# Moving the start addresses of an encoder kernel's SBUF tiles to multiples of 512 bytes

## The chip, the core and the metric

The kernel runs on one core of a Trainium2 chip. Five engines work side by side and are kept in step by semaphores: TensorE (PE in the profile, with its weight loads shown apart as PEld), VectorE (DVE), ScalarE (ACT), GpSimd (POOL) and SyncE (SP, which here only issues DMAs). TensorE reads two operands from SBUF, the on-chip memory of 128 partitions: a *stationary* operand of 128 columns, which a weight load brings in, and a *moving* operand of up to 512 columns, which is then streamed past it. The result goes to PSUM. The metric is the device time of one execution in microseconds, the median of several runs.

## The reference

Two layers over 512 positions of width 1024, in float32. Layer 0 mixes the positions with a stick-breaking attention, layer 1 with a gated linear recurrence (RG-LRU); each is followed by an MLP with a squared ReLU.

```python
for layer in range(2):
    h = rms_norm(x, norm_mix[layer])
    if layer == 0:
        y = stick_breaking_attention(h, w_qkv, w_o)   # 16 heads of 64
    else:
        y = rglru_block(h, w_in, conv_w, conv_b, w_a, b_a, w_x, b_x, lam, w_o)
    x = x + y
    h = rms_norm(x, norm_mlp[layer])
    u = relu(h @ w1[layer])                           # 1024 -> 4096
    x = x + (u * u) @ w2[layer]                       # 4096 -> 1024
return rms_norm(x, norm_final)
```

The attention weight of key k for query q is sigmoid(z) at k times the product of sigmoid(-z) over the keys between k and q. The recurrence is h[t] = a[t] h[t-1] + b[t] with gates computed from 16 diagonal blocks of 64 x 64. Nearly all of the arithmetic is in the dense products with the weight matrices.

## The kernel before

Activations lie with the features on the partitions: a chunk is 128 features by 512 positions, 8 chunks make the model width. Every float32 operand of a product is split into a high half, rounded to the TensorE format float32r, and a low half, the rest. A product is then three matmuls into the same PSUM bank: high times high, high times low, low times high (`three`, L217 to L221). ScalarE makes the high half of a weight tile (a cast, `wh`), VectorE the low half (a subtraction, `wl`), and DMAs on the SP queue, with some on POOL's, bring the raw weights.

The stages follow each other on TensorE in an order written out by hand. On the other engines a scheduler that works on estimated times sets the order of the instructions, save where the code chains them one behind the other. The stages are:

- Layer 0's mixer (to about 235 us): query and key projections with a moving operand of 512 positions (`xgh`, `xgl`, the halves of the normalised input) against weight slabs `wh`, `wl` (L219 to L221, L424); value projections in which the weight slab is the moving operand, 256 columns wide (L475 to L477); scores (`kh`, `kl` moving, `q` stationary, L559 and L560), transposes of the weights `w` with the identity as the moving operand (L600), values (`th`, `tl` moving, `v` stationary, L626 and L627); the output projection.
- The MLP of each layer by Strassen-Winograd's seven products in blocks, in four quarters. The quarters' *up* products (`Mlp.up`, L965) stream activations 256 columns wide past 128 columns of weights; the *down* products (`Mlp.times`, L1060) stream weights 512 columns wide past activations (`bh`, `bl`, or the split squares `sh`, `sl`). VectorE adds the block sums of weights, makes the low halves and gathers the results.
- Layer 1's mixer (about 566 to 720 us): input projections, convolution, gates, the scan on VectorE, the output projection.

SBUF is handed out by pools, in the order in which the pools are opened and, in a pool, in the order in which tags first occur. A tile starts on a multiple of 32 bytes. Pool `const` stands first; in it the one-column tile `eps_t` (L117) comes before the four 16 KB tiles `xgh`, `xgl`, `bh` and `bl`, and eight tiles of 8 columns (`lams`, L244) come behind them. `wpool` (raw weights, `wh`, `wl`), `work` (among others the small `rt`, `rc`, `rp`, `rn`, `rr`), `home`, and then the pools of each stage follow. So each small tile shifts the start of all that is allocated behind it:

| tiles | start, modulo 512 bytes, before | modulo 256 |
|---|---|---|
| `xgh`, `xgl`, `bh`, `bl` (every slice of them that a matmul takes) | 32 | 32 |
| `raw`, `wh`, `wl`, and all 2 KB tiles of `work` | 288 | 32 |
| `home` (also the tiles named `low`), `q`, `kh`, `kl`, `th`, `tl`, `v`, `w`; in layer 0's MLP `s41`, `sh`, `sl`; the gate weights | 480 | 224 |
| in layer 1's MLP `s41`, `sh`, `sl` (behind two small tiles of pool `last`) | 128 | 128 |
| `lasth`, `lastl` (behind the scan tiles, which are 513 columns wide) | 64 | 64 |
| `ones`, `ident` | 0 | 0 |

All slices that a matmul takes of a tile lie whole multiples of 512 bytes apart, so that each has its tile's number.

Of the kernel before, what the change touches and what calls it, by code (L numbers as in the profile page):

```python
# [11 lines left out]
F32 = mybir.dt.float32  # L12
F32R = mybir.dt.float32r
AF = mybir.ActivationFunctionType
# [3 lines left out]
P = 128  # L18
S = 512
D = 1024  # L20
C = D // P
# [40 lines left out]
def hybrid_encoder(  # L62
# [23 lines left out]
    nc = tc.nc  # L86
    V, A, G, PE = nc.vector, nc.scalar, nc.gpsimd, nc.tensor

    const = ctx.enter_context(tc.tile_pool(name="const", bufs=1))
    wpool = ctx.enter_context(tc.tile_pool(name="wpool", bufs=4))  # L90
    work = ctx.enter_context(tc.tile_pool(name="work", bufs=2))
# [5 lines left out]
    def bank(tag=None):  # L97
        if tag is None:
            tag = TAGS[turn[0] % len(TAGS)]
            turn[0] += 1  # L100
        return psum.tile([P, S], F32, tag=tag, name=f"ps_{tag}")

    def f(ap):
        return ap.bitcast(F32)
# [9 lines left out]
    V.memset(ones, 1.0)  # L114
    ident = const.tile([P, P], F32, tag="ident", name="ident")
    make_identity(nc, ident)
    eps_t = const.tile([P, 1], F32, tag="eps", name="eps_t")  # L117
    V.memset(eps_t, EPS)

    xgh = const.tile([P, C, S], F32R, tag="xgh", name="xgh")  # L120
# [5 lines left out]
    def halves(gname, c, xc):  # L126

        g = col(gname)[:, c : c + 1]
        A.activation(xgh[:, c, :], xc, AF.Identity, scale=g)
        return V.scalar_tensor_tensor(  # L130
            xgl[:, c, :], xc, g, f(xgh[:, c, :]), ALU.mult, ALU.subtract
        )
# [8 lines left out]
    class Squares:  # L141
# [21 lines left out]
        def inv_squares(self, ps):  # L163

            for t in range(S // P):
                PE.matmul(
                    ps[:, t : t + 1], self.acc[:, t * P : (t + 1) * P], ones[:, 0:1],
                    start=True, stop=True,
                )
            n = S // P  # L170
            rr = work.tile([P, 2 * n], F32, tag="rr", name="rr", bufs=1)
            V.tensor_scalar(rr[:, :n], ps[:, :n], 1.0 / D, EPS, ALU.mult, ALU.add)
            V.reciprocal(rr[:, :n], rr[:, :n])
            V.tensor_scalar(rr[:, n:], rr[:, :n], -1.0, None, ALU.mult)
            return rr
# [55 lines left out]
    def beside(ws, ah, al, pss, at, ks=range(C)):  # L231
# [9 lines left out]


    lams = {
        n: const.tile([P, C], F32, tag=f"lam_{n}", name=n)  # L244
        for n in ("ab", "pp", "den", "s1", "s2", "pl", "c8", "c4")
    }
    c8, c4 = lams["c8"], lams["c4"]
# [31 lines left out]
    NB = S // P  # L279
    PAIRS = H // 2  # L280
    half = [slice(0, HD), slice(HD, P)]
    so, early = {}, {}
# [7 lines left out]
    with ExitStack() as actx:  # L290
        hp = actx.enter_context(tc.tile_pool(name="hp", bufs=2))
        sp = actx.enter_context(tc.tile_pool(name="sp", bufs=1))
# [6 lines left out]
            fill=1.0, base=0, channel_multiplier=1,  # L299
        )  # L300

        scans = []
        for i in range(3):
            sc = sp.tile([P, S + 1], F32, tag=f"scan{i}", name=f"scan{i}")
            G.memset(sc[:, S : S + 1], 1.0)
            scans.append(sc)

        lasts = []
        for i in range(2):
            both = []  # L310
            for nm in ("h", "l"):
                t = sp.tile([P, 2 * P], F32R, tag=f"last{nm}{i}", name=f"last{nm}{i}")
                G.memset(f(t[:, :P]), 0.0)
                both.append(t)
            lasts.append(both)

        q, kh, kl, v, w = {}, {}, {}, {}, {}
        norm = {}
# [22 lines left out]
        def first_halves(pq, pk):  # L341

            qh, ql = parted(pq, "x")
            h = hp.tile([P, S], F32R, tag="th", name="th", bufs=3)
            l = hp.tile([P, S], F32R, tag="tl", name="tl", bufs=3)
            A.copy(h, pk)
            V.tensor_tensor(l, pk, f(h), ALU.subtract)
            q[0], kh[0], kl[0] = [], [], []
            for j in range(2):
                for tag, two, to in (("q", (qh, ql), q), ("kh", (h, h), kh), ("kl", (l, l), kl)):  # L350
                    t = hp.tile([P, S], F32R, tag=f"{tag}{j}", name=f"{tag}{j}")
                    for a, part in zip(half, two):
                        nc.sync.dma_start(out=f(t[a, :]), in_=f(part[half[j], :]))
                    to[0].append(t)
# [38 lines left out]
        others = {getattr(mybir.EngineType, e) for e in ("Activation", "DVE", "Pool", "SP")}  # L393
        with tc.manual_schedule(engines=others):
            A.dma_start(out=colt, in_=cols)
            A.activation(work.tile([P, 1], F32, tag="rt", name="early"), eps_t, AF.Sqrt)
            for j in range(2):
                parts[j][2](1, A)
            for c in range(C):
                nc.sync.dma_start(out=xcs[c], in_=xT[:, c, :])  # L400
                if c in (0, 3, 5):
                    for j in range(2):
                        parts[j][2]((c + 1) // 2)
            for j in range(2, 6):
                for i in range(2):
                    parts[j][2](i)

            parts[0][3](0, V.tensor_copy)
            for kind, c in START:
                if kind == "x":  # L410
                    halves("mix0", c, xcs[c])
                elif (kind, c) == ("q", 0):
                    parts[0][3](c, None)
                elif kind != "s":
                    parts["qknm".index(kind)][3](c)
                else:
                    A.activation(sqs[c], xcs[c], AF.Square)
                    if c:
                        V.tensor_tensor(sums, sums, sqs[c], ALU.add)

            for k in range(C):
                for n, (low, y) in enumerate(((0, xgh), (0, xgl), (1, xgh))):
                    for i in range(2):
                        PE.matmul(  # L424
                            first[i], parts[i][low][:, k, :], y[:, k, :], start=k == n == 0,
                            stop=k == C - 1 and n == 2,
                        )
            first_halves(*first)

        def inverse():  # L430

            pc = bank("z")
            for t in range(NB):
                PE.matmul(
                    pc[:, t : t + 1], sums[:, t * P : (t + 1) * P], ones[:, 0:1],
                    start=True, stop=True,
                )
            rc, rp, rn = (work.tile([P, NB], F32, tag=n, name=n, bufs=1) for n in ("rc", "rp", "rn"))
            diag = work.tile([P, S], F32, tag="sq", name="diag")
            with tc.high_priority():  # L440
                norm["root"] = A.activation(rc, pc[:, :NB], AF.Sqrt, bias=eps_t, scale=1.0 / D)
                V.reciprocal(rc, rc)
                for t in range(NB):
                    ts = slice(t * P, (t + 1) * P)
                    V.tensor_scalar(diag[:, ts], ident, rc[:, t : t + 1], None, ALU.mult)
                V.tensor_scalar(rp, rc, SCALE, None, ALU.mult)
                V.tensor_scalar(rn, rc, -SCALE, None, ALU.mult)
            norm.update(rc=rc, rp=rp, rn=rn)
            yield
            pr = bank("z")  # L450
            PE.matmul(pr, ones, diag, start=True, stop=True)
            r = work.tile([P, S], F32, tag="r", name="r")
            with tc.high_priority():
                norm["copy"] = A.copy(r, pr)
            norm["r"] = r
            yield
# [921 lines left out]
    with ExitStack() as rctx:  # L1378
# [155 lines left out]
        def root(c):  # L1534
            OA.activation(om[c], om[c], AF.Sqrt)
# [18 lines left out]
        def out_low(c):  # L1554
# [4 lines left out]
            "N": rms, "r": inverse, "R": gate_raw, "W": gate_high, "X": gate_low, "G": gates,  # L1559
            "n": scaled, "b": first_tap, "t": taps, "h": high, "l": low, "s": sigmoids,  # L1560
            "m": gated_input, "T": tanh, "E": exp, "d": decay, "q": root, "k": recur,
            "z": gate, "g": gelu, "y": times_gate, "u": out_high, "i": out_low,
        }
# [21 lines left out]
    with ExitStack() as mctx:  # L1585
        lp = mctx.enter_context(tc.tile_pool(name="last", bufs=1))
# [26 lines left out]

        A.activation(lp.tile([P, 1], F32, tag="rt", name="early"), eps_t, AF.Sqrt)

        ss = lp.tile([P, NB, 3], F32, tag="ss", name="ss")
        bias = lp.tile([P, NB], F32, tag="bias", name="bias")

        def square(t, h, i, cols=slice(0, S), end=False):
# [17 lines left out]
            EG.tensor_tensor(y, y, gb[h][:, cols], ALU.mult)  # L1637

        def root(t, i):
            rt = work.tile([P, 1], F32, tag="rt", name="rt")  # L1640
            A.activation(rt, ss[:, t, i : i + 1], AF.Sqrt, bias=bias[:, t : t + 1], scale=1.0 / D)
            V.reciprocal(rt, rt)
            return rt
# [24 lines left out]
        def end(ws, xs):  # L1668
            EG.turn(True)
            for t in range(2):  # L1670
                square(t, 0, 0)
                scaled(t, 0)
                square(t, 1, 1, end=True)
                rt = root(t, 1)
                one(t, 0, rt)
                both(t, 1, rt, last=mlp.gained)
# [6 lines left out]
            mlp.collect("P4", 0, xs[0])  # L1683
            square(2, 0, 1, end=True)
            two = root(2, 1)
            mlp.collect("P4", 1, xs[1])
            parts = [slice(i * HS, (i + 1) * HS) for i in range(2)]
# [86 lines left out]
```

## Time and profile before

| what | value |
|---|---|
| median of 3 runs | 1043.36 us (1043.2 to 1043.92) |
| span of the profiled execution | 1041.3 us, so the median lies 2.1 us above it |
| TensorE busy | 1032.1 us, 99% of the span, 5862 matmul records |
| VectorE, ScalarE, GpSimd busy | 858.7 us, 702.3 us, 171.8 us |
| granted TensorE clock, mean | 0.999 |
| HBM read | 137.41 MB |

The page gives no own time of the profiled execution beside its span. A matmul's record is longer than its turn on the engine: records overlap, since the next one begins to stream while the last one drains. The 512-column matmuls have records of about 390 ns but begin 227 to 234 ns apart. How long TensorE is held is therefore read from starts: from the chain of work, whose pieces give a start, a length and a count, or from the busy time of one source line over the whole span, divided by its count.

### The profile page before, as it was taken

The numbers are of one execution on the slowest core, as the hardware profiler recorded it, in microseconds if no ns is written. First come the engines' busy times: TensorE is split into PE (matmuls) and PEld (weight loads), VectorE is DVE, ScalarE is ACT, GpSimd is POOL, SyncE is SP. The second block draws the span as 40 slices with busy tenths as digits, with TensorE's granted clock in tenths as the row PEclk, the third lists the DMA queues.
The fourth block names the chain that finished last, engine by engine and source line by source line (L and its number), as shares of the span: only waits on it lengthen the run. The fifth ranks groups of instructions, "written<-read, shape, count | busy, mean of one in ns | idle before, by whom it ended". The sixth has DMA issues, their size and how long they took to land.

```text
span 1041.3 us, 15858 instructions
## 1 busy us (share of the span) xinstructions
PE 1032.1 (99%) x5862; PEld 902.2 (87%) x5862; DVE 858.7 (82%) x1148; ACT 702.3 (67%) x1083; POOL 171.8 (17%) x239
## 2 busy tenths in 40 slices
PE   9999999999999999999999999999999999999997
PEld 7988888888888988988988888888888988988986
DVE  7888787848788898898899888984789797897897
ACT  6777676826766773773775799964755773773865
POOL 0444444420010010010011121200000010010012
PEclk9999999999999999999999999999999999999999
DMA  7745454528546667567682675453346667667663
GB/s 243 216 111 143 117 151 102 162 88 297 137 81 189 182 137 211 161 136 209 162 209 76 159 176 142 102 222 101 82 87 173 180 138 206 161 137 200 145 129 107
DMA packets 53260, 160.46 MB, mean 154 GB/s; under 512 B 6720, under 2 KB 8256, under 8 KB 53184
## 3 DMA queue, kind: packets, MB, share of 16 engines
q1 hardware_dynamic: 42096, 120.35, 35.5%
q0 software_dynamic: 10656, 38.80, 22.5%
q8 instruction: 46, 0.75, 0.3%
q10 hardware_dynamic: 432, 0.31, 0.1%
q14 instruction: 30, 0.25, 0.1%
HBM read 137.41 MB, written 4.19 MB: 136 GB/s over the span
## 4 chain that ended last, share of the span: by engine, by line
PE 96%; ACT 2%; DMA 1%; DVE 1%; issue 0%; POOL 0%; ACTq 0%; DVEq 0%
PE ps_t L1060 17%; PE ps_acc L965 10%; PE ps_acc L1060 8%; PE ps_z L965 8%; PE ps_acc L221 5%; PE ps_acc L219 5%; PE ps_acc L220 5%; PE ps_o L965 5%; PE ps_z L1060 4%; PE ps_t L219 2%; PE ps_t L220 2%; PE ps_t L221 2%; PE ps_o L219 2%; PE ps_o L220 2%; PE ps_o L221 2%; PE ps_z L221 2%
## 5 line engine op out<-in xcount | busy, mean ns | idle before, releaser
L754 ACT CAST wh<-b 128x1024 fp32r<-128x1024 f32 x168 | 174.1, 1047 | 126.1 <-DVE b L754 71.5
L754 DVE TENSOR_TENSOR wl<-b,wh 128x1024 fp32r<-128x1024 f32 x168 | 203.5, 1220 | 48.4 <-ACT wh L754 47.9
L1042 POOL DMA_DIRECT2D b<-in_w_dn x40 | 35.0, 874 | 364.3 <-DVE b L754 204.4
L219 PE MATMUL ps_acc<-xgh,wh 128*128 128x512 f32 x192 | 78.5, 409 | 0.0
L221 PE MATMUL ps_acc<-xgl,wh 128*128 128x512 f32 x192 | 75.2, 391 | 0.0
L220 PE MATMUL ps_acc<-xgh,wl 128*128 128x512 f32 x192 | 75.1, 391 | 0.0
L578 DVE TENSOR_TENSOR_SCAN scan<-keep,later 128x128 f32<-128x128 f32 (+1 forms) x64 | 59.9, 939 | 16.9 <-ACT keep L568 9.8
L214 DVE TENSOR_TENSOR wl<-raw,wh 128x512 fp32r<-128x512 f32 (+2 forms) x70 | 61.5, 906 | 14.9 <-ACT wh L212 14.8
L754 ACT ACTIVATE u<-u 128x512 f32<-128x512 f32 x100 | 63.1, 632 | 5.5 <-DVE u L754 3.8
L212 ACT CAST wh<-raw 128x512 fp32r<-128x512 f32 (+2 forms) x70 | 50.6, 758 | 20.6 <-PE ps_acc L221 7.3
L582 POOL TENSOR_TENSOR w<-w,scan 128x128 f32<-128x128 f32 (+1 forms) x64 | 51.9, 812 | 56.7 <-DVE scan L578 53.3
L1042 POOL DMA_DIRECT2D b<-in_w_up x24 | 20.8, 868 | 240.2 <-DVE b L754 71.8
L754 DVE TENSOR_TENSOR b<-b,b 128x1024 f32<-128x1024 f32 x48 | 58.7, 1222 | 1.3
L754 DVE TENSOR_TENSOR u<-u 128x512 f32<-128x512 f32 (+1 forms) x92 | 54.8, 596 | 2.7 <-ACT u L754 1.1
L965 PE MATMUL ps_z<-xgh,wh 128*128 128x256 f32 x192 | 54.2, 282 | 0.0
L965 PE MATMUL ps_z<-xgh,wl 128*128 128x256 f32 x192 | 54.1, 282 | 0.0
L754 ACT CAST wh<-raw 128x1024 fp32r<-128x1024 f32 x46 | 48.0, 1047 | 8.7 <-PE ps_acc L1060 6.7
L965 PE MATMUL ps_acc<-low,wh 128*128 128x256 f32 x192 | 53.9, 281 | 0.0
L1060 PE MATMUL ps_t<-wl,sh 128*128 128x512 f32 x126 | 50.1, 398 | 0.0
L1060 PE MATMUL ps_t<-wh,sh 128*128 128x512 f32 x126 | 49.7, 395 | 0.0
L1060 PE MATMUL ps_t<-wh,sl 128*128 128x512 f32 x126 | 49.5, 393 | 0.0
L1060 PE MATMUL ps_t<-wh,bh 128*128 128x512 f32 x126 | 49.3, 391 | 0.0
(399 smaller groups left out, 3420.7 us busy)
## 6 DMA issues: line engine op xcount, KB each, us to landing
b<-in_w_dn SPq DMA_DIRECT2D x48, 512.0 KB, 4.4
b<-in_w_dn POOLq DMA_DIRECT2D x40, 512.0 KB, 5.7
b<-in_w_up SPq DMA_DIRECT2D x36, 512.0 KB, 4.5
b<-in_w_up POOLq DMA_DIRECT2D x24, 512.0 KB, 5.5
raw<-in_w_m SPq DMA_DIRECT2D x16, 512.0 KB, 4.5
raw<-in_w_dn SPq DMA_DIRECT2D x16, 512.0 KB, 4.7
raw<-in_w_in SPq DMA_DIRECT2D x16, 512.0 KB, 3.8
raw<-in_w_qk SPq DMA_DIRECT2D x12, 512.0 KB, 3.7
```

Source lines behind the costliest of these rows:

```text
L212: A.copy(wh[:, k, :], raw[:, k, :])
L214: V.tensor_tensor(wl[:, k, :], raw[:, k, :], f(wh[:, k, :]), ALU.subtract)
L219: PE.matmul(ps, wh, ah, start=start, stop=False)
L220: PE.matmul(ps, wl, ah, start=False, stop=False)
L221: PE.matmul(ps, wh, al, start=False, stop=stop)
L578: V.tensor_tensor_scan(sc[:, S - n : S][:, ::-1], keep[:, :n][:, ::-1], later[:, S - n :][:, ::-1], 1.0, ALU.mult, ALU.max,)
L582: G.tensor_tensor(wt, wt, sc[:, S - n + 1 : S + 1], ALU.mult)
L754: ins = getattr(self.e, name)(*args, **kwargs)
L965: PE.matmul(ps[:, i * HS : (i + 1) * HS], m, y, start=new and i == k == n == 0, stop=i == 1 and k == C // 2 - 1 and n == 2, skip_group_che ...
L1042: G.dma_start(out=unit[b].rearrange("p j n -> p (j n)"), in_=unit["src"](to), accum_op=ALU.add)
L1060: PE.matmul(ps, m, y[:, jj, cols], start=first and n == 0, stop=last and n == 2, skip_group_check=not new,)
```

## The change

A pool `small` is opened ahead of `const` and takes the small tiles: `eps_t`, the eight `lams`, `rt`, `rc`, `rp`, `rn`, `rr`. `eps_t` is made 16 columns wide, of which the first is used, and `ss` in the last stage 104 columns wide, of which the first 12 are used; both widths only fill up the pool to a multiple of 512 bytes at which the next tile begins. The 513-column scan tiles are allocated behind `lasth` and `lastl` and not in front of them. In the built program every operand of every matmul, moving or stationary, then starts on a multiple of 512 bytes: each number of the table above becomes 0. No size of a computation, no buffer count and no wait changes.

```diff
+    small = ctx.enter_context(tc.tile_pool(name="small", bufs=1))
     const = ctx.enter_context(tc.tile_pool(name="const", bufs=1))
...
-    eps_t = const.tile([P, 1], F32, tag="eps", name="eps_t")
+    eps_t = small.tile([P, 16], F32, tag="eps", name="eps_t")[:, :1]
...
-            rr = work.tile([P, 2 * n], F32, tag="rr", name="rr", bufs=1)
+            rr = small.tile([P, 2 * n], F32, tag="rr", name="rr")
...
     lams = {
-        n: const.tile([P, C], F32, tag=f"lam_{n}", name=n)
+        n: small.tile([P, C], F32, tag=f"lam_{n}", name=n)
...
-        scans = []
-        for i in range(3):
-            sc = sp.tile([P, S + 1], F32, tag=f"scan{i}", name=f"scan{i}")
-            G.memset(sc[:, S : S + 1], 1.0)
-            scans.append(sc)
-
         lasts = []
...
                 both.append(t)
             lasts.append(both)
+
+        scans = []
+        for i in range(3):
+            sc = sp.tile([P, S + 1], F32, tag=f"scan{i}", name=f"scan{i}")
+            G.memset(sc[:, S : S + 1], 1.0)
+            scans.append(sc)
...
-            A.activation(work.tile([P, 1], F32, tag="rt", name="early"), eps_t, AF.Sqrt)
+            A.activation(small.tile([P, 1], F32, tag="rt", name="early", bufs=2), eps_t, AF.Sqrt)
...
-            rc, rp, rn = (work.tile([P, NB], F32, tag=n, name=n, bufs=1) for n in ("rc", "rp", "rn"))
+            rc, rp, rn = (small.tile([P, NB], F32, tag=n, name=n) for n in ("rc", "rp", "rn"))
...
-        ss = lp.tile([P, NB, 3], F32, tag="ss", name="ss")
+        ss = lp.tile([P, 104], F32, tag="ss", name="ss")[:, : 3 * NB]
+        ss = ss.rearrange("p (t i) -> p t i", t=NB)
...
-            rt = work.tile([P, 1], F32, tag="rt", name="rt")
+            rt = small.tile([P, 1], F32, tag="rt", name="rt", bufs=2)
```

The one place where instructions move is POOL at the program's start, where it fills tiles with constants. On PE, DVE, ACT and SP the instructions and their order are the same in both kernels. Before, POOL's row from the fill of `later` (the mask of later keys) to the first multiplication by a scan stood so:

```order
L296 MEMSET later_100 128x512
L305 MEMSET scan0_105 128x1
masks.py:199 ISA
masks.py:199 AFFINE_SELECT ident_70<-ident_70 128x128
L305 MEMSET scan1_107 128x1
L305 MEMSET scan2_109 128x1
L313 MEMSET lasth0_111 128x128
L313 MEMSET lastl0_113 128x128
L313 MEMSET lasth1_115 128x128
L313 MEMSET lastl1_117 128x128
L297 AFFINE_SELECT later_100<-later_100 128x128
```

In the changed kernel the same stretch of POOL's row is:

```order
L297 MEMSET later_103 128x512
L308 MEMSET lasth0_108 128x128
masks.py:199 ISA
masks.py:199 AFFINE_SELECT ident_73<-ident_73 128x128
L308 MEMSET lastl0_110 128x128
L308 MEMSET lasth1_112 128x128
L308 MEMSET lastl1_114 128x128
L315 MEMSET scan0_116 128x1
L315 MEMSET scan1_118 128x1
L315 MEMSET scan2_120 128x1
L298 AFFINE_SELECT later_103<-later_103 128x128
```

The three one-column fills of the scan tiles now stand behind the four fills of `lasth` and `lastl`, and the identity is made one fill later; the row is of the same length.

## The prediction

> **What bounds the kernel now.** I read the page first, then the waits, the chain of work, and last the rows in order of time inside steady stretches.
>
> ```profile
> span 1041.3 us, 15858 instructions
> ...
> PE 1032.1 (99%) x5862; PEld 902.2 (87%) x5862; DVE 858.7 (82%) x1148; ACT 702.3 (67%) x1083; POOL 171.8 (17%) x239
> ...
> PE 96%; ACT 2%; DMA 1%; DVE 1%; issue 0%; POOL 0%; ACTq 0%; DVEq 0%
> ```
>
> TensorE is busy for 99% of the span and is 96% of the chain. Its own waits are these three:
>
> ```profile
> PE ps_acc L424 <- ACT xgh L129: 1.1, 1, 1.1
> PE ps_z L381 <- DVE eps_t L118: 1.1, 1, 1.1
> PE ps_z L965 <- ACT u L754: 0.6, 1, 0.6
> ```
>
> They come to 2.8 us, so the end is set by the sum of the matmuls' turns. The change touches those turns alone: where operands start. Is a turn's length a matter of the start? Pieces of the chain (start, us, what and how many) in six steady stretches, in each of which all moving operands and all stationary ones have the same two starts:
>
> ```profile
> 330.56 2.52 PE ps_acc L965 x21
> ...
> 333.56 2.27 PE ps_acc L965 x20
> ...
> 800.59 4.64 PE ps_acc L965 x39
> ...
> 772.73 2.49 PE ps_t L1060 x11
> ...
> 470.12 2.06 PE ps_acc L1060 x9
> ...
> 775.22 2.57 PE ps_t L1060 x11
> ```
>
> Divided by their counts, with the starts (modulo 256 bytes) of moving and stationary operand behind:
>
> - 256 columns: 120.0 ns (32 and 32, `xgh` past `wh`); 113.5 (224 and 32, layer 0's `s41` and `low` past `wh`); 119.0 (128 and 224 by turns, and 32, the same lines in layer 1)
> - 512 columns: 226 ns (32 and 32, `wh` past `bh`); 229 (32 and 224, `wh` past layer 0's `sh`); 234 (32 and 128, `wh` past layer 1's `sh`)
>
> The same source line, with the same shapes and with nothing to wait for, runs 113.5 or 119.0, 229 or 234, as its tiles lie. So the start matters, by 3 to 6% of a turn; the tiles' order in memory is a term of the time.
>
> What is the term made of? At equal starts (32 and 32) the two sizes differ by 226.5 - 120.0 = 106.5 ns for 256 columns, 0.416 ns a column; what is left is 13.3 ns a matmul, at both sizes the time of 32 columns. At 224 and 32 the rest is 113.5 - 106.5 = 7 ns, the time of 16 columns. Sixteen float32 columns are 64 bytes. An operand that begins 32 bytes past a multiple of 64, as all moving operands in these rows but layer 1's `s41` do, reaches into one 64-byte piece more than its length needs, 33 for 32 or 17 for 16. I read the 7 ns as that piece, and the second 7 ns as the moving stream meeting the weight load, since the next weights are read in the same time:
>
> ```profile
> 330.64 0.28 PE L965 MATMUL ps_acc<-xgh,wh 128*128 128x256 f32 x1
> 330.64 0.19 PEld L965 LDWEIGHTS ps_acc<-xgh,wl 128*128 128x128 f32 x1
> ```
>
> That reading is an inference from the six pieces. No stretch has both operands on a multiple of 64, so the state after the change isn't in this trace. The nearest thing is the transposes, whose moving operand `ident` starts at 0 (128 columns of float32, stationary `w` at 224):
>
> ```profile
> 59.05 0.60 PE L600 MATMUL ps_t<-ident,w 128*128 128x128 f32 x4
> ...
> L600 PE MATMUL ps_t<-ident,w x160: 270/272/327, 50.3 to 228.5; 128*128 128x128 f32 x160
> ```
>
> Four of them in 0.60 us, of which the last takes 0.272: (0.60 - 0.272) / 3 = 109 ns each. If float32 streams at half the rate, that is 106.5 ns and a rest of 2.5, well under 7.
>
> **The change part by part.** *Moving the small tiles to the front* adds and removes no instruction; their readers are the same. A column tile's start could matter to VectorE and ScalarE, but neither is waited for, beyond 0.6 us at L965. *Behind the scan tiles*, POOL's fills change places at the program's start:
>
> ```profile
> 1.42 0.10 POOL L305 MEMSET scan<- 128x1 f32 x1
> ...
> 2.44 0.29 POOL L297 TENSOR_SCALAR_AFFINE_SELECT later<-later 128x128 f32<-128x128 f32 x1
> 32.17 0.29 POOL L572 TENSOR_SCALAR_AFFINE_SELECT w<-w 128x128 f32<-128x128 f32 x1 [29.44 <-ACT w L567]
> ```
>
> All fills are over by 2.7 us and POOL then idles for 29.44 us. ScalarE's first write to a scan tile is a square made from `x`, after the first chunk has come; the fills keep their sum, so this costs nothing. Without that cover it would be the 0.2 us of a fill or two. *DMAs* land at other addresses in the same order; between 30 us and the last stage TensorE waits for none.
>
> *Every matmul's start* is the whole of the term. TensorE's time by line over the span, and for L219 to L221 the first and last of fifteen turns:
>
> ```profile
> 0.00:1041.30 1041.30, 239.53 (x2016) 239.18 (x2016) 1.00 0.58 154
> ...
> 0.00:1041.30 1041.30, 311.16 (x1356) 252.24 (x1356) 1.00 0.58 154
> ...
> 18.58 0.23 PE ps_t L219
> ...
> 21.98 0.23 PE ps_t L219
> ...
> L475 PE MATMUL ps_acc<-wh,xgh 128*128 128x256 f32 x112 | 32.4, 289 | 0.0
> ```
>
> The first row is L965 alone (2016 turns, 118.8 ns), the second L1060 alone (1356, 229.5 ns); 21.98 - 18.58 over 15 is 226.7 ns for the 3 x 496 projections; the value projections (3 x 112 of the last row's kind) have the first piece's starts, 120.0 ns.
>
> What do they cost at starts of 0 and 0? From below: the fixed part falls to the transposes' 2.5 ns, 109 and 216 ns. From above: nothing of the fixed part is tied to the piece, and equal starts are the worst relation, 120 ns and, by the worst steady piece, 234. I take the middle, by the row that the new state is nearest to: 32 and 32, the one with equal starts. It loses its extra piece (7 ns) and keeps its meeting with the weight load (6.7): 113.3 and 220.0 ns. Then:
>
> - L1060: 1356 x (229.5 - 220.0) = 12.9 us
> - L219 to L221: 1488 x (226.7 - 220.0) = 10.0 us
> - L965: 2016 x (118.8 - 113.3) = 11.1 us
> - L475 to L477: 336 x (120.0 - 113.3) = 2.3 us
>
> Together 36.3 us; scores, values and transposes, some 500 turns with smaller or unknown differences, are left out.
>
> Who is late next? VectorE, in the down products. Two such stages, and an up stage ahead of them (PE, PEld, DVE, ACT, POOL busy):
>
> ```profile
> 330.00:370.00 40.00, 40.00 (x340) 39.88 (x340) 33.09 (x35) 31.46 (x42) 3.48 (x4) 1.00 0.63 159
> 370.00:408.00 38.00, 38.00 (x168) 31.09 (x167) 35.76 (x41) 19.89 (x25) 4.35 (x5) 1.00 0.77 186
> ...
> 838.00:877.00 39.00, 39.00 (x172) 31.69 (x171) 36.30 (x42) 20.67 (x26) 4.37 (x5) 1.00 0.76 184
> ```
>
> At 220 ns the second takes 38.0 x 220.0 / 229.5 = 36.4 us, and VectorE's 35.76 are 98% of it. I charge 0.3 us of stalls to each of the seven full down stages, 2 us. The profiled execution's span of 1041.3 becomes 1007; the median lies 2.1 us above that span, so the forecast is 1043.4 - 36.3 + 2 = **1009 us**.
>
> **The rivals.** *The whole rest goes.* At 216 and 109.2 ns the same four lines give 18.3 + 15.9 + 19.4 + 3.6 = 57 us. But a down stage can't become shorter than VectorE's work in it: 38.0 - 35.76 = 2.2 us is to be had in each, about 13 us of L1060's 18.3 less some stalls. 50 us are left, 993. For it speaks the transposes' row, against it that they stream slower and so meet the weight load less. The Trainium skill, page "TensorE: Matmul & The Clock Gate", section "Wait — 56ns, not 53.3ns?", has this as the rule for back-to-back matmuls: columns over 2.4 GHz and about 2.5 ns more, 215.7 ns at 512. The trace agrees on the slope (0.416 ns a column) and disagrees on the rest, which is 7 to 20 ns in the six pieces; by that rule the time would be this rival's.
>
> *Nothing changes*: only the distance between the two operands counts, not where they start. Equal starts are what 32 and 32 is already; then all goes to 226.7 and 120.0. L1060 gains 1356 x 2.8 = 3.8 us, L965 loses 2016 x 1.2 = 2.4, the other lines stand: 1042. For it speaks that the most frequent relation of before has equal starts; against it the next rows. The Trainium skill, page "SBUF — State Buffer", section "Specifications (TRN2)", gives lines of 16 bytes, each new one at a price. All starts of before are multiples of 32 already, so by that rule there is nothing to align. The trace disagrees, since the layout modulo 256 moves the turn by 5 ns.
>
> *It becomes slower*: with equal starts both streams ask for the same place at once, and 32 and 32 escapes it only by its half piece. Four matmuls in a row at 224 and 224 (values and scores, 512 columns):
>
> ```profile
> 54.80 0.23 PE ps_o L626
> 55.03 0.24 PE ps_o L627
> 55.27 0.23 PE ps_z L559
> 55.50 0.23 PE ps_z L560
> ```
>
> (55.50 - 54.80) / 3 = 233 ns at equal starts, not 226. At 233 and 120 the lines lose 1356 x 3.5 + 1488 x 6.3 + 2016 x 1.2 = 4.7 + 9.4 + 2.4 = 16.5 us: 1060. It decides if the mean turn of 512 columns comes out above its present (311.16 + 1488 x 0.2267) / 2844 = 228.0 ns with the 256-column ones unmoved. Against it: those four stand in a mixed stretch, and their moving operands cut a 64-byte piece as well.
>
> **How the numbers follow.** Forecast (piece gone, meeting stays, 1000 to 1020): 0.36. Rest gone as well (985 to 1000): 0.27. Nothing changes (1038 to 1046): 0.12. Slower (1046 to 1062): 0.25. What a measurement can tell from no change is 0.2%, 2 us; of the third case I count about half as that, the rest as faster or slower by a little. So faster 0.67, same 0.06, slower 0.27. The range 988 to 1053 leaves out the lowest tip of the second case and more than half of the last, some 0.2. Over the two faster cases alone it would be 988 to 1020.
>
> **What would show it.** Right: L219 to L221 begin 220 ns apart, L965 113 ns, and layer 1's down products run like layer 0's; the chain's pieces in each stage are of one cadence; VectorE is above 95% in the down stages, with single waits of TensorE on `wl` at L1060. If the turns are 216 and 109, the rest went too. If they are 227 and 120, only the distance counts. If 512 columns take 233 or more, equal starts collide. The forecast is wrong above all if my 64-byte piece is not what the 7 ns are, or if VectorE or ScalarE can't follow.

## The result

The time does not change. After: 1043.24 us, median of 12 runs (1042.33 to 1045.25). Before, on the same chip: 1043.48 us (1041.54 to 1044.43). The ratio of after to before is 1.0003, with a 95% interval of 0.9994 to 1.0011. The forecast of 1009 us is 34 us too low.

The page of the profile after has the same head as before:

```profile
span 1042.4 us, 15858 instructions
...
PE 1032.3 (99%) x5862; PEld 906.2 (87%) x5862; DVE 859.0 (82%) x1148; ACT 701.6 (67%) x1083; POOL 172.5 (17%) x239
...
PE 89%; DVE 4%; DMA 2%; ACT 2%; issue 2%; POOL 0%; SPq 0%; ACTq 0%; DVEq 0%; POOLq 0%
```

TensorE is still busy for 99% of the span. (The chain now leads through VectorE and a DMA for part of the way, because it follows a few short waits of TensorE at the MLP's lines; none of them is long.) Those waits, and TensorE's time by line over the whole span for L966 (L965 of before, the up products) and for L1061 (L1060 of before, the down products):

```profile
PE ps_acc L425 <- ACT xgh L130: 1.2, 1, 1.2
PE ps_z L382 <- DVE eps_t L119: 1.1, 1, 1.1
PE ps_z L966 <- ACT u L755: 1.0, 1, 1.0
PE ps_acc L966 <- ACT u L755: 0.2, 1, 0.2
```

```profile
0.00:1042.40 1042.40, 243.37 (x2016) 242.82 (x2016) 1.00 0.59 154
...
0.00:1042.40 1042.40, 307.46 (x1356) 252.29 (x1356) 1.00 0.59 154
```

The down products have gained 311.16 - 307.46 = 3.70 us, and the up products have lost 243.37 - 239.53 = 3.84 us. The two cancel. So the change does move the turns, in both directions. The chain shows how; here is one up stage and the down stage behind it, as it was before the change:

```profile
330.45 13.98 PE ps_acc L965 x120
...
353.06 2.74 PE ps_o L965 x24
...
358.62 2.72 PE ps_o L965 x24
...
389.22 5.48 PE ps_acc L1060 x24
```

and the same places after it:

```profile
330.92 14.39 PE ps_acc L966 x120
...
353.95 2.88 PE ps_o L966 x24
...
359.71 2.88 PE ps_o L966 x24
...
390.30 5.44 PE ps_acc L1061 x24
```

Before, a turn of 256 columns took from 2.72 / 24 = 113.3 to 120 ns, as its tiles lay; after, the steady ones take 2.88 / 24 = 14.39 / 120 = 120 ns. Before, a turn of 512 columns took 226 to 234 ns (the prediction's pieces of 11 turns; the piece shown, 5.48 / 24 = 228.3 ns, has half of its turns past `bh` and half past `sh` and `sl`); after, 5.44 / 24 = 226.7 ns. There is one cadence, that is one steady time from start to start, for each size, except that behind a wait some eight to eleven turns of 512 columns take 224 to 236 ns. It is the cadence that 32 and 32 had before: the slowest of 256 columns and the fastest of 512. Most projections had it already, at 226.7 ns. (The table ahead of the prediction leaves out the weights in pool `wmore`, which started at 224; 186 of the 1488 projection turns take them and ran at 229 ns in steady stretches.) The projections' three lines add up to nearly the same TensorE time as before (586.9 and 587.1 us). The scores and values took 233 ns before and are faster too; their starts in order of time, L627 being L626 of before:

```profile
55.18 0.39 PE L627 MATMUL ps_o<-th,v 128*128 128x512 f32 x1
...
56.09 0.39 PE L220 MATMUL ps_acc<-xgh,wh 128*128 128x512 f32 x1
```

Four turns (two values, two scores) in 0.91 us, 227 ns each. (Their two starts were equal before as well, 224 and 224. In the run with the weights moved by 64 bytes, below, they have equal starts too, but stand between projections whose two starts differ; there the same four take 0.92 us, 230 ns each, and so do the four of before when the last of them is counted in. So a short group of turns seems to depend also on what stands around it.)

### The profile page after: what moved, and what is told of

The parts are those of the page before. It is cut to its first block, busy times and chain, and to the rows that moved or that the text cites. A ratio compares the mean times of both kernels' runs of the same rounds, so it can differ in the third digit from the quotient of the medians.

```text
span 1042.4 us, 15858 instructions
## 1 busy us (share of the span) xinstructions
PE 1032.3 (99%) x5862; PEld 906.2 (87%) x5862; DVE 859.0 (82%) x1148; ACT 701.6 (67%) x1083; POOL 172.5 (17%) x239
## 4 chain that ended last, share of the span: by engine, by line
PE 89%; DVE 4%; DMA 2%; ACT 2%; issue 2%; POOL 0%; SPq 0%; ACTq 0%; DVEq 0%; POOLq 0%
PE ps_t L1061 14%; PE ps_acc L966 8%; PE ps_z L966 8%; PE ps_acc L1061 7%; PE ps_o L966 5%; PE ps_acc L220 5%; PE ps_acc L222 5%; PE ps_acc L221 5%; PE ps_z L1061 4%; PE ps_t L220 2%; PE ps_t L222 2%; PE ps_t L221 2%; PE ps_o L220 2%; PE ps_o L222 2%; PE ps_o L221 2%
## 5 line engine op out<-in xcount | busy, mean ns | idle before, releaser
L221 PE MATMUL ps_acc<-xgh,wl 128*128 128x512 f32 x192 | 75.1, 391 | 0.0
L966 PE MATMUL ps_z<-xgh,wh 128*128 128x256 f32 x192 | 54.3, 283 | 0.0
L966 PE MATMUL ps_z<-xgh,wl 128*128 128x256 f32 x192 | 54.3, 283 | 0.0
L966 PE MATMUL ps_acc<-low,wh 128*128 128x256 f32 x192 | 54.3, 283 | 0.0
L1061 PE MATMUL ps_t<-wl,sh 128*128 128x512 f32 x126 | 49.2, 391 | 0.0
L1061 PE MATMUL ps_t<-wh,bh 128*128 128x512 f32 x126 | 49.2, 390 | 0.0
L1061 PE MATMUL ps_t<-wl,bh 128*128 128x512 f32 x126 | 49.1, 390 | 0.0
L1061 PE MATMUL ps_t<-wh,sh 128*128 128x512 f32 x126 | 49.0, 389 | 0.0
```

The costliest lines, as they stand in the source:

```text
L221: PE.matmul(ps, wl, ah, start=False, stop=False)
L966: PE.matmul(ps[:, i * HS : (i + 1) * HS], m, y, start=new and i == k == n == 0, stop=i == 1 and k == C // 2 - 1 and n == 2, skip_group_che ...
L1061: PE.matmul(ps, m, y[:, jj, cols], start=first and n == 0, stop=last and n == 2, skip_group_check=not new,)
```

## The experiments

Two theories stood against each other. By the first, the forecast's, what counts is where an operand *starts*: an operand that begins 32 bytes past a multiple of 64 costs an extra piece. By the second only the *distance* counts, the start of the moving operand less that of the stationary one, modulo 256 bytes. After the change all distances are 0. The experiments move tiles by unused tiles, or read a longer tile from a later column, and leave no computation out. That an operand "cuts" a 64-byte piece means that it begins in the middle of one.

### Moving the weights by 64, 32, 96 and 128 bytes

The weight tiles (`raw`, `wh`, `wl`) are pushed on by an unused tile ahead of them, and what lies behind them is brought back to a multiple of 256 by a second one. Modulo 256 the weights are then the only operands that don't start at 0. (Those in pool `wmore`, which 62 of the 496 projections of a line take, stay at 0.) They are the stationary operand in up products and projections (distance 256 less the shift) and the moving one in down products (distance equal to the shift). For 64 bytes:

```diff
     bl = const.tile([P, C, S], F32R, tag="bl", name="bl")
+    const.tile([P, 16], F32, tag="shift", name="shift")
...
     work = ctx.enter_context(tc.tile_pool(name="work", bufs=2))
+    work.tile([P, 48], F32, tag="back", name="back", bufs=1)
```

The others have 8 and 56, 24 and 40, 32 and 32 columns. Expected of 64 bytes:

> The changed kernel with the pool of weight tiles (raw, wh, wl) begun 64 bytes further on and the next pools put back, so that up products and projections have a distance (start of the moving operand less start of the stationary one, modulo 256 bytes) of 192, down products and value projections of 64. If the distance alone sets the turn: L968, the up products, 113.5 ns instead of 120 (192 took 113.5 before), L1063, the down products, 229 instead of 227 (64 took 229 before), so 2016 x 6.5 less 1356 x 2 = 10 us faster, about 1033, and less if 192 is also good for 512 columns. If what counts is whether an operand cuts a 64-byte piece: nothing cuts one, so 227, 120 and 1043 as in the changed kernel.

of 32:

> The same with the weight tiles begun 32 bytes further on: distance 224 for up products and projections, 32 for down products and value projections. Distance alone: both values are new; by their neighbours (0 and 192 gave 120 and 113.5, 0 and 64 gave 227 and 229) the up products between 113 and 120, the down products 227 to 229, 1030 to 1045. 64-byte pieces: every weight tile now cuts one, so 7 ns more in the down products and value projections, where they move, 234 and 127, some 12 us slower, 1055.

of 96:

> Weight tiles begun 96 bytes further on: distance 160 for up products and projections, 96 for down products and value projections. Distance alone: 512 columns at 160 took 234 before, so the projections L222 to L224 go from 227 to 234 (434 x 3 x 7 = 9 us slower); 256 columns at 96 took about 118 to 119, so the value projections gain 1 ns; up at 160 and down at 96 are new. 64-byte pieces: as with 32 bytes, down products 234, projections 227.

of 128:

> Weight tiles begun 128 bytes further on: distance 128 everywhere between weights and activations. Distance alone: a new value, either side of 227 and 120; if 256 bytes is a ring of places and both streams walk it at the same speed, this is the farthest apart they can be and the least they can meet, down to 220 and 113 (30 us faster, 1013). If the ring is 128 bytes it is the same as 0: 227, 120, 1043. 64-byte pieces: 227, 120, 1043.

Measured, in one run each beside a run of before at 1043.65 us: 1046.40 (64 bytes), 1051.42 (32), 1054.71 (96), 1054.00 (128). TensorE's time of the up products' line and the down products' line; with 64 bytes

```profile
0.00:1060.00 1060.00, 233.25 (x2016) 231.97 (x2016) 1.00 0.56 151
...
0.00:1060.00 1060.00, 313.14 (x1356) 251.62 (x1356) 1.00 0.56 151
```

and with 32 bytes

```profile
0.00:1060.00 1060.00, 239.80 (x2016) 239.46 (x2016) 1.00 0.56 151
...
0.00:1060.00 1060.00, 315.21 (x1356) 251.97 (x1356) 1.00 0.56 151
```

At 64 bytes no operand cuts a 64-byte piece, just as in the changed kernel, and by the first theory no turn should move. But the up products become 10.1 us shorter and the down products 5.7 longer. At 32 bytes the weights do cut a piece, and the up products still become 3.6 us *shorter*. The first theory can explain neither. The cadences are in the chain; in the run with 64 bytes:

```profile
857.26 5.60 PE ps_t L1063 x24
...
882.46 10.92 PE ps_acc L968 x96
...
946.50 5.49 PE ps_t L1063 x24
...
960.24 14.13 PE ps_acc L968 x120
```

10.92 / 96 = 113.8 ns at distance 192, the fast cadence that layer 0's `s41` and `low` had before at 224 and 32, which is the same distance. The distance explains it; the starts are others. (The last two rows come back below.)

The expected total of 1033 us was missed by 13. What ate it: the down products, at 229 or 233 ns, lose 5.7 us, and the projections' three lines lose 5.9 (592.8 us after 586.9), since 512 columns at distance 192 take 233 ns. 10.1 gained and 11.6 lost; the span is 2.2 us longer than that of the changed kernel. Some of it, inside these lines' times too, is waiting. The weight loads, which wait in the matmuls' place, show it:

```profile
PEld ps_z L968 <- ACT u L757: 3.1, 5, 1.7
PEld ps_t L1063 <- DVE wl L757: 2.7, 5, 0.6
PEld ps_z L1063 <- DVE wl L757: 1.8, 6, 0.4
```

With 96 bytes the two lines take 238.98 and 315.31 us, with 128 bytes 242.55 and 314.50. So a distance of 128, the farthest apart that two starts can be, is no remedy: 512 columns take 5.57 / 24 = 232 ns there, 256 columns 118.6 to 120.

### The same distances, other starts

An unused tile of 32 bytes stands first in `const`, so that every operand begins 32 bytes on. All of them cut a 64-byte piece again, and all distances stay 0:

```diff
     const = ctx.enter_context(tc.tile_pool(name="const", bufs=1))
+    const.tile([P, 8], F32, tag="shift", name="shift")
```

> The changed kernel with everything behind pool small begun 32 bytes further on: every operand starts at 32 modulo 512, every distance stays 0. Distance alone: 227 and 120 ns as in the changed kernel, 1043. If the start itself counts, by the 64-byte piece of the prediction (each operand now cuts one more): 234 and 127, 30 us slower.

Measured: 1043.15 us. The chain in the stage shown above:

```profile
325.27 5.44 PE ps_t L1062 x24
330.71 14.39 PE ps_acc L967 x120
```

The cadences are those of the changed kernel to the last digit, 226.7 and 119.9 ns. With every piece cut nothing is dearer. This ends the first theory: the start by itself does not count.

### Distances between the multiples of 32

`xgh` and `xgl` are made 64 columns longer and read from four columns, 16 bytes, behind their start on; `ss` is narrowed from 104 to 40 columns to keep to the room. The same with 52 columns gives a distance of 208.

```diff
-    xgh = const.tile([P, C, S], F32R, tag="xgh", name="xgh")
-    xgl = const.tile([P, C, S], F32R, tag="xgl", name="xgl")
+    xgh, xgl = (
+        const.tile([P, C * S + 64], F32R, tag=t, name=t)[:, 4 : 4 + C * S].rearrange(
+            "p (c s) -> p c s", c=C
+        )
+        for t in ("xgh", "xgl")
+    )
```

> The changed kernel with xgh and xgl read 16 bytes further on in tiles 64 columns longer: distance 16 for 368 of the projections of a line and 1056 up turns, 240 for the value projections, 0 elsewhere. If distance acts in steps of 32 bytes, nothing moves: 227 and 120. If it acts smoothly or in steps of 16: between the values at 0 and 32, 227 to 233 and 117 to 120.

> The changed kernel with xgh and xgl read 208 bytes further on: distance 208 for 368 of the projections of a line and 1056 up turns, 48 for the value projections. Distance in steps of 16 or smoothly: up turns between those at 192 and 224, 114 to 118; projections 233. If only multiples of 64 differ from each other, up turns 113.5 as at 192.

Measured: 1046.93 us with 16 bytes, beside 1043.41 of before, and 1047.47 with 208, beside 1043.12. Up turns with 16 bytes, from the chain:

```profile
351.86 2.85 PE ps_z L970 x24
```

2.85 / 24 = 118.8 ns, and the projections at the same distance take 231.6 ns by their starts. Sixteen bytes matter, then, so the grain is finer than a piece of 32 or 64. At 208 the two sizes take 119.2 and 234.1 ns. I had expected 114 to 118 for the up turns, between its neighbours' values; as far as one run shows, the dip at 192 is a narrow one.

What all runs together give for the mean turn in undisturbed steady stretches, in ns:

| distance of moving from stationary start, modulo 256 | 256 columns | 512 columns |
|---|---|---|
| 0 | 119.9 | 227.3 |
| 16 | 118.8 | 231.6 |
| 32 | 116.9 | 233.3 |
| 64 | 117.1 (two stretches of 113.4) | 229.8 (stretches of 229 and of 233) |
| 96 | 119.7 | 233.4 |
| 128 | 118.6 in some stretches, 120 in others | 232.5 |
| 160 | 117.9 | 234.1 |
| 192 | 113.5 in some stretches, 118 in others | 233.3 |
| 208 | 119.2 | 234.1 |
| 224 | 118.3 | 233.1 |

Distance 0 is the best that was found for 512 columns and, with 96 and some stretches of 128, the worst for 256. The rows other than 0, 64 and 192 rest on one or two kernels each. That the distance counts modulo 256 rests on two comparisons: `xgh` and its weights lay 256 bytes apart modulo 512 before (32 and 288) and 0 apart after, with the same 120 and 226.7 ns; at 128 bytes apart, 512 columns take 232.5.

### Distance 0 for the down products alone

If this table is right, the kernel of before should gain when only its layer-dependent down products (distances 160 and 64) go to 0, and its up products keep theirs. An unused tile ahead of `sh` and `sl` does it, 16 columns in layer 0 and 40 in layer 1:

```diff
                 else:
+                    if not self.gap:
+                        self.gap = True
+                        self.bp.tile([P, (16, 40)[self.layer]], F32, tag="gap", name="gap", bufs=1)
                     self.a[p] = [
```

> The kernel before with one part of the change alone: in the MLPs sh and sl are moved by a gap tile to 32 modulo 256, where bh, bl and the weight tiles are, so that every down product has distance 0 (start of the moving operand less start of the stationary one, modulo 256 bytes); the up products keep the distances of before. If the change is a sum of two opposite shares by distance: the 1332 down turns of 512 columns give the 3.5 us that they gave in the changed kernel, the up turns stand, ratio 0.997, 1040. If the two shares only seemed to cancel, and the end is set by something that doesn't follow the turns (the weights' preparation on VectorE, say): 1043, with the gain come back as stalls at L1063.

Measured: 1041.61 us against 1043.41, a ratio of 0.9983, interval 0.9974 to 0.9992: faster, by 1.8 us. The down products' line:

```profile
0.00:1060.00 1060.00, 308.28 (x1356) 252.03 (x1356) 1.00 0.57 151
```

2.9 us less than before's 311.16, with the up line unmoved at 239.79. A part of the gain in turns comes back as waiting for the weights' low halves. Before had 1.2 us of it on `ps_t`, and now it is

```profile
PEld ps_t L1063 <- DVE wl L754: 1.8, 5, 0.5
```

### The table's best for both sizes

Now distance 0 for most turns of 512 columns and 192 for most of 256. (Left over are 128 of the 496 projections of a line, which are at 192, and the value projections and 192 of the 2016 up turns, which are at 0.) The weights, `bh`, `bl`, `sh`, `sl` and the gate weights start at 64; `xgh` and `xgl` have two views, one at 0 for the MLP and one at 64 for the mixers:

```diff
+    (mixh, mixl), (xgh, xgl) = (
+        [t[:, a : a + C * S].rearrange("p (c s) -> p c s", c=C) for t in both] for a in (16, 0)
+    )
...
     home = ctx.enter_context(tc.tile_pool(name="home", bufs=1))
+    home.tile([P, 48], F32, tag="gap", name="gap")
...
+                        self.bp.tile([P, 16], F32, tag="gap", name="gap", bufs=1)
...
     wmore = wctx.enter_context(tc.tile_pool(name="wmore", bufs=2))
+    wmore.tile([P, 16], F32, tag="gap", name="gap", bufs=1)
```

> Built from the distances: 0 for 512 columns, 192 for 256. Weight tiles, bh, bl, sh, sl, wmore and the gate weights begin at 64 modulo 256; xgh and xgl are read at 0 by the MLPs and at 64 by the two mixers (two views of one tile, 16 columns longer); home, s41 and low are at 0. So down products and 354 of 496 projections a line are at 0, 1824 of 2016 up turns at 192, and the first MLP products (128 a line) at 192 with 512 columns, where 233 instead of 227 ns were seen. Distance alone: 1824 x 5.5 = 10 us gained, 384 x 6 = 2.3 us lost against the changed kernel, 1036 without stalls; with stalls like the 3.9 us of the run with 64 bytes 1039; ratio to the kernel before 0.993 to 0.996. If stalls take all that the turns give, 1043.

Measured: 1042.85 us, a ratio of 0.9995 (0.9986 to 1.0003), no change that can be told. The expected 1036 us is missed by 7. One piece of the chain says why:

```profile
330.96 14.13 PE ps_acc L977 x120
```

14.13 / 120 = 117.8 ns: 104 of these turns are at distance 192 and 16 (those that move `bh` or `bl`) at 0, and by their starts none of the stretches at 192, here or in the other stages, is in the fast cadence. At 113.5 the 1824 up turns at 192 would take 1824 x 4.3 = 7.8 us less. The down turns do take 226.7 ns, as they should. So distance 192 has two cadences at 256 columns. The run with the weights at 64 bytes, looked at again, has both on the same line with the same tiles: 113.8 and 117.8 ns in the two up rows quoted there.

Does the stage ahead decide which one comes? In that run the down turns ahead ran at distance 64, in this one at 0. So `sh` and `sl` were put back to 0 (the last gap but one taken out), which gives half of the down turns distance 64 again:

> The kernel built from the distances, but with sh and sl left at 0, so that the 666 down turns with them have distance 64, among them the last before each up stage. In that kernel all up turns at distance 192 took 118 ns, in the run with weight tiles 64 bytes on nearly all took 113.5, at the same distance. If a stretch at 192 has two steady states and keeps the one in which it is entered, and the turns ahead of it decide that, these up turns take 113.5 again: 1824 x 4 = 7.3 us gained, 666 x 2.5 = 1.7 us lost against that kernel, 1037, ratio to the kernel before 0.994. If the difference lies in something else (the start modulo 512, say), 118 and 1044.

Measured: 1043.82 us against 1043.12, a ratio of 1.0009 (1.0001 to 1.0018). The up turns stay slow, except between 829 and 840 us. That stretch (up line, busy time and count) and a later one:

```profile
829.00:840.00 11.00, 11.00 (x99) 11.00 (x99) 1.00 0.53 187
882.00:917.00 35.00, 35.00 (x300) 35.00 (x299) 1.00 0.64 166
```

From starts it is 113.5 ns in the first and 117.8 in the second. The theory that the turns ahead alone decide falls. What the traces do show is that a stretch keeps its cadence until TensorE has to wait, and that it can be another one behind a wait: here behind one of 0.9 us at 826 us, in the run with 64 bytes from 113.5 to 118 behind one of 1.7 us at 827. Other waits changed nothing, such as one of 0.6 us at 356 us in that run. Which of the two comes isn't explained by any run here.

### Down products at 0, and layer 1's up products at 192

One more step from the kernel of before: the gap of 16 columns in both layers, and `ss` 40 columns wide, which puts layer 1's MLP tiles where layer 0's are (`s41` at 224, distance 192, in place of 128, distance 96).

```diff
+                        self.bp.tile([P, 16], F32, tag="gap", name="gap", bufs=1)
...
-        ss = lp.tile([P, NB, 3], F32, tag="ss", name="ss")
+        ss = lp.tile([P, 40], F32, tag="ss", name="ss")[:, : 3 * NB]
+        ss = ss.rearrange("p (t i) -> p t i", t=NB)
```

> The run with the down products alone in line, and beside it layer 1's MLP pools moved from 128 to 224 modulo 256, so that its s41 and low stand to the weight tiles as layer 0's do (distance 192 instead of 96). Distance alone: the down turns at 227 as there, and layer 1's up turns as layer 0's (117.5 instead of 118.9 ns on average of the first ten products of a stage), 1008 x 1.4 = 1.4 us more gained; ratio to the kernel before 0.997, 1040. If the gain is given back as stalls it stays at the 0.998 of that run.

Measured: 1040.57 us against 1043.12, a ratio of 0.9978 (0.9969 to 0.9987). It beats both kernels, by 2.6 us. (Against the down products alone, 0.9983, the intervals overlap.) Up line and down line:

```profile
0.00:1060.00 1060.00, 238.40 (x2016) 237.87 (x2016) 1.00 0.57 151
...
0.00:1060.00 1060.00, 308.74 (x1356) 251.95 (x1356) 1.00 0.57 151
```

1.1 and 2.4 us less than before. And its waits, where before had 1.2 and 0.8:

```profile
PEld ps_t L1063 <- DVE wl L754: 2.3, 6, 0.5
PEld ps_z L968 <- ACT u L754: 1.9, 1, 1.9
```

Of 3.5 us in turns the span of the profiled execution shows 1.6 (1039.7 after 1041.3); some 2 us went to these waits. That execution took 1041.55 us and is one of the kernel's slower ones, so the median one, 2.6 us faster than before, lost less. When TensorE's turns become shorter here, VectorE and ScalarE are late at single places.

## Why the prediction was wrong

- *TensorE bounds the kernel, and a turn depends on where its tiles lie*: right. The layout moves a turn of 256 columns between 113.5 and 120 ns, one of 512 between 226.7 and 234. But the difference is no fixed part of a matmul beside a slope of 0.416 ns a column. At distance 0 the two sizes differ by 226.7 - 119.9 = 106.8 ns, 0.417 a column; at 192 by 233.3 - 113.5 = 119.8, 0.468. What saves 6.4 ns at 256 columns costs 6.6 at 512, so the 7 ns that were found at 256 columns could not be taken off the turns of 512.
- *The step that failed* is the one that costs the new state: "It loses its extra piece (7 ns) and keeps its meeting with the weight load (6.7): 113.3 and 220.0 ns." At starts of 0 and 0 the turns are 120 and 226.7 ns, as at 32 and 32; with all operands 32 bytes on they are so again. There is no 64-byte piece in the turn. The inference behind it changed two things at a time: the pieces of before with the shorter turns (224 and 32) differed from those with the longer (32 and 32) both in the start of the moving operand and in its distance from the stationary one. As the stationary `wh` started at 32 in all rows of 256 columns, start and distance were one and the same variable there, and these rows could not tell one from the other. Nor had any of them shown the piece: 224 and 32 both cut one, and layer 1's `s41`, which at 128 cuts none, was not faster. (The row of 119.0 also holds turns in which `bh` moves; ahead of them, by their starts, 22 turns of `s41` and `low` took 118.6 ns on average, where the sum would give some 113.)
- *The sum*: -12.9 us for L1060 measured -3.70; -11.1 for L965 measured +3.84, the sign reversed; -10.0 for L219 to L221 and -2.3 for L475 to L477 measured 0.2 or less, as their distance was 0 before already, but for 186 turns at 64. The +2 for stalls isn't there either, since no stage became shorter by much: of the down stage from 370 us, 38.0 us long, VectorE is busy for 35.88, 94%.
- *The fills on POOL, the small tiles, the DMAs at nothing*: right as far as the trace shows. The span grew by 1.1 us; TensorE reaches the first stretch in steady run (25 us) 0.5 us later, about what two executions of one kernel differ by. No wait on a fill is among TensorE's waits.
- *VectorE is late next*: not tested by the change, which made no stage shorter by enough. In the experiments that did, it came true in size: 1 to 2 us more of waiting, on `wl` and on ScalarE's `u`.
- *The rivals.* "Nothing changes: only the distance counts" is what happened, in the total (1042 forecast) and in its parts (L1060 3.8 us gained and 3.70 measured, L965 2.4 lost and 3.84 measured). L965 lost more than forecast because the 118.8 ns of before, busy time over count, has waits and the ends of the last records in it: by their starts the undisturbed up turns took 118.2 ns before and 120.0 after, 3.6 us over 2016 turns. I gave it a chance of 0.12 with the argument that the layout modulo 256 moves the turn, which speaks against "nothing to align" but not against "only the distance counts". One rival held two theories, and the evidence against the one was charged to the other. The rule on 16-byte lines that was named there (the Trainium skill, page "SBUF — State Buffer", section "Specifications (TRN2)") gives the right total for this change, but by a path that the runs don't bear out: by it no layout of before would differ from another, and they do by 7 ns.
- "The whole rest goes" (993 us) is refuted at all distances tried: no steady stretch of any run came below 113 or 226 ns. "Equal starts collide" (1060 us) is refuted for 512 columns, where equal starts are the fastest (226.7 ns in every full stage), and half true for 256, where they are the slowest, at 120 ns; but this was known from 32 and 32 and priced there. That 1043 us lies inside the stated range of 988 to 1053 is luck: the range reached so far up for the sake of this rival, which did not come about.

What stays open: by which mechanism the distance acts (that the stream meets the weight load is argued, not shown, since no run here took the weight load away); whether it is the distance to the matmul's own stationary operand or to the next one, which are the same in every steady stretch; and what selects between the two cadences, to which the value and score turns' 233 and 227 ns at distance 0 may belong.

## What to carry to other kernels

If TensorE is the bound and its turns differ on one line, sort the steady pieces of the chain by the *difference* of the two operands' starts modulo 256 bytes, one size of the moving operand at a time, and move one tile alone before laying out all of them alike; a layout that is best for 512 columns was the worst for 256. An inference from the trace that a start costs something should name a pair of rows in which nothing but this start differs, and if there is none, the theory that the other quantity does it deserves as much of the chance. A few nanoseconds a turn are worth having only as far as the engines that feed TensorE can follow: here about half of what the fastest kernel gained in turns came back as waits in its profiled execution.

## What was not expected of the hardware

- The size of the effect is not the same for both widths of the moving operand, and not even its sign: 192 bytes apart is the fastest for 256 columns (113.5 ns) and among the slowest for 512 (233.3).
- One and the same line with the same tiles has two steady cadences at some distances: 113.8 and 117.8 ns at 192, 233 and 229 ns at 64 (rows `857.26` and `946.50` above). At 192 one was seen to follow the other behind a wait of TensorE, but not behind every wait. Even at distance 0 a wait of 0.09 us at 777 us in the changed kernel is followed by eight turns of 224 to 236 ns, 231.5 on average, before 226.7 ns come back.
- The Trainium skill, page "TensorE: Matmul & The Clock Gate", section "Step-by-step: what each phase is for", has two independent read ports for the moving operand and the weight load, so that the load of the next weights takes nothing from the stream. The runs here don't agree with it in full: a turn of the same size, with the same weight load beside it, changes by 3 to 6% with the distance between the two operands and not with their common start. That the two reads share bandwidth is an inference from this, not shown.
